# A two-layer decoder trunk: score products of two heads in the two row halves of TensorE, and SwiGLU products grouped by width

## The chip, the cores and the metric

The program runs on one core of one Trainium2 chip. The metric is the device time of one execution in microseconds (us); less is better. Every time below is taken from the runs or from the hardware profile of the kernel before the change.

## What is computed

Two consecutive decoder layers over 256 positions and a model width of 1024. Layer 0 mixes block-sparse and dilated attention, layer 1 uses a three-branch attention (compressed, selected blocks, sliding window); after each attention come a SwiGLU block and a gated per-layer embedding. The part that the change touches:

```python
def _swiglu(x, wg, wu, wd):
    return (jax.nn.silu(x @ wg) * (x @ wu)) @ wd

# layer 1, 16 query heads in 4 groups, head width 64
q  = _rms(_heads(q, NSA_HEADS), qn)
ks = _rms(_heads(ks, NSA_GROUPS), kn_s)
kw = _rms(_heads(kw, NSA_GROUPS), kn_w)
s  = einsum('bghsd,bgkd->bghsk', q, k) * ATTN_SCALE + bias   # for each branch
pr = softmax(s, causal)
o  = gates[0] * o_cmp + gates[1] * o_slc + gates[2] * o_win
h  = h + o @ w_out
h  = h + _swiglu(_rms(h, norm_ffn), w_gate, w_up, w_down)
```

With 256 positions all blocks are selected, so the selected and the window branch are two causal attentions with their own keys.

## The kernel before, in words

**Precision.** Every large product is made from two halves of each operand: a number is split into `hi` (rounded to the matmul's fast 32-bit form) and `lo` (the rest), and hi·hi + hi·lo + lo·hi is summed in PSUM. Weights are loaded by SyncE in units of 512 KB into six `raw` buffers; ScalarE writes `hi`, VectorE (in layer 1 for half of some units GpSimd) writes `lo` (`emit_load`, `emit_split`, lines 98 to 130). `take` (line 189) hands a unit to the products and starts later loads and splits.

**Order of the work.** The TensorE and SyncE queues are written by hand: the program text walks through the projections in order, and after every few products `tick` (line 158) lets queued generators (`push`) place a step of side work: the norm chains, the transposes of q and k, and `attend` (line 664), which places the three parts of attention. When each may be placed is set by a model clock and by the table `KN` of delays. The queues of VectorE, ScalarE and GpSimd are ordered by the framework's scheduler. Each queue runs in order, so a step of side work that isn't ready holds everything behind it.

**Layer 1 attention.** `q_split` and `k_split` (lines 864 to 886) normalise 8 heads at a time: `norm_twice` writes every head twice side by side, `split_t` transposes 128 columns of this at a time (128x128 transposes into the tile `qps`), so that both partition halves hold the same head, and writes q as hi over lo on the 128 partitions (`QS`) and two forms of k (`KK`). `attn1` (line 999) then has three parts. `A(i)` makes all scores of one head: two products with 256 columns (queries 0 to 127) and two with 512 (queries 128 to 255), each over all 128 rows of the array; VectorE adds the bias and takes the maximum (`neg_scores`, line 474), ScalarE takes the exponential, VectorE and GpSimd scale. `B(i)` transposes the probabilities of one head (six 128x128 transposes, tile `t`), ScalarE or VectorE copies them out of PSUM. `C(k)` makes the outputs of a pair of heads (tile `o`, 20 recorded products). `cmp_scores(b)` (line 965, tile `cs`) makes the compressed-branch scores of 8 heads. Heads 0 to 7 go first, then heads 8 to 15, whose attention waits until output pair 3 is out. The filler between these steps is the rest of the input projection (`ic`, products of 512, 304 or 256 columns), the embedding projection (`pa`) and the output projection (`oc`, 192 products of 256 columns in layer 1, of which 48 wait for the last output pair).

**SwiGLU.** `mm_units_t` and `block_step` (lines 234 to 255): for a block of 128 output features the hi weights meet hi and lo of the input side by side (one product of 512 columns) and then the lo weights meet hi (256 columns), into the same PSUM bank. The two alternate. `ga` is the gate, `ua` the up, `da` the down projection; there are 1024 such pairs in the two layers. Layer 0's scores (`attn0`, tile `s`) already use 64-row products in the two row halves, in plain 32-bit, each recorded as two passes.

Of the kernel before, what the change touches and what calls it, by code (L numbers as in the profile page):

```python
# [35 lines left out]
KN = {'stF': 7.12, 'stP': 6.0, 'st0': 1.48, 'st1': 11.0, 'sq': 3, 'LSb': 2, 'warm': 4, 'spF': 6.77, 'spP': 5.23, 'burst': 6, 'prep0': 2.6, 'prep1': 2.0, 'qk': 11.39, 'qk2': 12.0, 'qk3': 9.53, 'qk4': 13.44, 'ev': 0.63, 'gap0': 1.54, 'gap1': 2.4, 'LB0': 7.35, 'LB1': 7.66, 'LC': 2.13, 'hT': 5.0, 'cmp': 12.0, 'ev1': 1.5, 'c0': 4.0, 'c00': 0.5, 'c1': 4.5, 'c2': 9.0, 'ns': 'PPVV', 'lop': 2, 'ptd': 1, 'pb': 1}  # L36
# [3 lines left out]
def trunk(ctx: ExitStack, tc: tile.TileContext, a, out):  # L40
# [20 lines left out]
    def big(i, dt):  # L61
        return fix.tile([128, (16, 16, 12)[i] * S], dt, tag=f"big{i}", name=f"big{i}")
# [26 lines left out]
    def plan(name, w, k0, nk, c0, N):  # L89

        pieces = [(c0, N)] if isinstance(c0, int) else c0
        rows = w[k0 * 128:(k0 + nk) * 128].rearrange("(k p) n -> p k n", p=128)
        units.append((name, [(rows[:, :, c:c + n], n) for c, n in pieces], nk, sum(n for _, n in pieces)))
# [4 lines left out]
    def emit_load():  # L98
        i = ws["ld"]
        if i >= len(units):  # L100
            return
        _, aps, nk, N = units[i]
        r = wp.tile([128, 1024], F32, tag="raw", name="raw", bufs=NRAW)
        raws[i] = r
        c = 0
        for ap, n in aps:
            nc.sync.dma_start(out=r[:, :nk * N].rearrange("p (k n) -> p k n", k=nk)[:, :, c:c + n], in_=ap)
            c += n
        ws["ld"] += 1
# [124 lines left out]
    def block_step(ks, k, b, blk, x, kx, start, stop):  # L234
# [3 lines left out]
        if c is None:  # L238
            mm(t[:, 0:2 * S], hi, both.rearrange("p e s -> p (e s)"), start, False)
            mm(t[:, S:2 * S], lo, both[:, 0, :], False, stop)  # L240
        else:
            o = t[:, c:c + S]
            mm(o, hi, both[:, 0, :], start and c == 0, False)
            mm(o, hi, both[:, 1, :], False, False)
# [74 lines left out]
    plan_out(a["w_out_nsa"][0])  # L319
# [38 lines left out]
    def load_tb(tb, i):  # L358
        nc.sync.dma_start(out=tb[:, 4 * i:4 * i + 4], in_=a["tb"][:, 4 * i:4 * i + 4])
# [186 lines left out]
    def ffn(l, slot):  # L546
        nslot = 1 - slot
        hh = [big(i, F32R).rearrange("p (f e s) -> p f e s", e=2, s=S) for i in range(3)]

        def hh_pair(f, e):  # L550

            return hh[f // 8][:, f % 8:f % 8 + 2, e, :]

        def hh_both(f):
            return hh[f // 8][:, f % 8]
# [108 lines left out]
    def attend(n, A, B, C, gap, lb, p0, ready=(), pb=3, ptb=4, per_pt=1, per_a=1):  # L664

        tA, tB, k = [], [], 0
        while 2 * k < n:
# [18 lines left out]
    big0, big1, big2 = (big(i, F32) for i in range(3))  # L686
    qT = big0[:, 0:2048].rearrange("p (a s) -> p a s", s=S)
    kT = big0[:, 2048:4096].rearrange("p (a s) -> p a s", s=S)
    TB = big1.rearrange("p (h j) -> p h j", h=16)
# [21 lines left out]
    def attn0(h0):  # L711
# [4 lines left out]
        def A(k):  # L716
# [10 lines left out]
            for e, x0, x1, n in parts:  # L727
                neg_scores(p[:, e, x0:x1], s[e][:, x0:x1], TB[:, 2 * pr + e, 256 - (x1 - x0):256], nm[:, n:n + 1])
# [46 lines left out]
    def dil_bias(i):  # L775
        load_tb(TB, i)
        for k in range(4 * i, 4 * i + 4, 2):
            nc.gpsimd.tensor_tensor(TB[:, k:k + 2, :], TB[:, k:k + 2, :], lc[:, None, :].to_broadcast([128, 2, 256]), op=OP.add)
# [4 lines left out]
    load_tb(TB, 0)  # L783
    load_tb(TB, 1)
# [17 lines left out]
    QS = big(0, F32R).rearrange("p (h s) -> p h s", s=S)  # L802
    KK = big(1, F32R).rearrange("p (e g b s) -> p e g b s", e=2, g=4, b=2)
# [9 lines left out]
    KCT = fix.tile([128, 4, 2, 16], F32R, name="kct")  # L813
    TB = []

    def load_tb1():

        t = wk.tile([128, 2, 256], F32, tag="tb", name="tb", bufs=4)
        nc.sync.dma_start(out=t, in_=a["tb"][:, 2 * len(TB):2 * len(TB) + 2])
# [18 lines left out]
    def norm_twice(accs, mul):  # L838
# [3 lines left out]
        for b in range(2):  # L842
            for t in range(2):
                q = wk_tile("qn")
                src = accs[t][:, b * 256:b * 256 + 256].rearrange("p (h d) -> p h d", d=64)
                nc.vector.tensor_tensor(q.rearrange("p (h e d) -> p h e d", e=2, d=64),
                                        src[:, :, None, :].to_broadcast([128, 4, 2, 64]),
                                        comb[:, t, 4 * b:4 * b + 4, None, None].to_broadcast([128, 4, 2, 64]), op=OP.mult)
                res.append(q)
        return res  # L850

    def split_t(qn, h, gcol, hi, lo_at, lo):

        p = st_tile("qps")
        for e in range(2):
            for t in range(2):
                tr(p[:, e * 256 + t * 128:e * 256 + (t + 1) * 128],
                   qn[2 * (h // 4) + t][:, (h % 4 + e) * 128:(h % 4 + e) * 128 + 128])
# [3 lines left out]
        nc.vector.scalar_tensor_tensor(lo, pv[lo_at:], g[lo_at:], hi[lo_at:].bitcast(F32), op0=OP.mult, op1=OP.subtract)  # L862

    def k_split(accs):

        kn = norm_twice(accs, 1.0)

        def gen():
            for h in range(0, 8, 2):
                br, g = h // 4, h % 4  # L870
                split_t(kn, h, 5 + br, KK[:, 0, g:g + 2, br, :], 0, KK[:, 1, g:g + 2, br, :])
                yield KN["ev"] if g else 0.0
# [3 lines left out]
    def q_split(accs, h0):  # L876

        qn = norm_twice(accs, 64.0)

        def gen():  # L880
            for h in range(0, 8, 2):
# [6 lines left out]
    def compress(idr):  # L888
# [71 lines left out]
        pv = bass.AP(tensor=p.tensor, offset=p.offset, ap=[p.ap[0], [15, 4], [1, 16]])  # L960
        nc.scalar.activation(KCT[:, :, 0, :], pv, AF.Identity, scale=g)
        nc.vector.scalar_tensor_tensor(KCT[:, :, 1, :], pv, g, KCT[:, :, 0, :].bitcast(F32), op0=OP.mult, op1=OP.subtract)
        ev["kc"] = clk[0] + 0.8

    def cmp_scores(b):
        if b == 0:
            nc.gpsimd.memset(PC, 0.0)
        p = st_tile("cs")
        pv = p.rearrange("p (t h e c) -> p t h e c", t=2, h=8, e=2)
        for i in range(8):  # L970
            hd = 8 * b + i
            for t in range(2):
                mm(pv[:, t, i], QS[:, hd, t * 128:(t + 1) * 128], KCT[:, hd // 4], start=True, stop=True)
# [4 lines left out]
        nc.vector.tensor_tensor(sc, pv[:, :, :, 0, 0:15], tcv[:, :, 8 * b:8 * b + 8, :], op=OP.add)  # L978
        nc.vector.tensor_tensor(sc, pv[:, :, :, 1, 0:15], sc, op=OP.add)
# [19 lines left out]
    def attn1(h0):  # L999
# [3 lines left out]
        def A(i):  # L1003
            hd = h0 + i
            g = hd // 4
            s0, s1 = st_tile("s0"), st_tile("s1")
            for e in range(2):
                mm(s0[:, 0:256], QS[:, hd, 0:128], KK[:, e, g, :, 0:128], start=e == 0, stop=e == 1)
            for e in range(2):
                mm(s1, QS[:, hd, 128:256], KK[:, e, g], start=e == 0, stop=e == 1)  # L1010
            p = wk.tile([128, 768], F32, tag="p", name="p1", bufs=3)
            nm, l, r = small("nm", (128, 4)), small("l", (128, 4)), small("rl", (128, 4))
            for n, (x0, x1) in enumerate(cuts):
                src = s0[:, x0:x1] if n < 2 else s1[:, x0 - 256:x1 - 256]
                neg_scores(p[:, x0:x1], src, TB[hd // 2][:, hd % 2, 256 - (x1 - x0):256], nm[:, n:n + 1])
            if hd % 2 and len(TB) < 8:
                load_tb1()
            for n, (x0, x1) in enumerate(cuts):
                nc.scalar.activation(p[:, x0:x1], p[:, x0:x1], AF.Exp, bias=nm[:, n:n + 1], scale=-1.0,  # L1019
                                     accum_out=l[:, n:n + 1])  # L1020
            nc.vector.reciprocal(r, l)
            nc.vector.tensor_tensor(r.rearrange("p (t b) -> p t b", t=2), r.rearrange("p (t b) -> p t b", t=2), G[:, :, hd, 1:3], op=OP.mult)
            for n, (x0, x1) in enumerate(cuts):
                if KN["ns"][n] == "A":
                    nc.scalar.activation(p[:, x0:x1], p[:, x0:x1], AF.Copy, scale=r[:, n:n + 1])
                    continue
                e = nc.gpsimd if KN["ns"][n] == "P" else nc.vector
                e.tensor_scalar(p[:, x0:x1], p[:, x0:x1], r[:, n:n + 1], None, op0=OP.mult)
            stt["p", i] = p
# [14 lines left out]
        def C(k):  # L1044
            pts = [stt.pop(("pt", 2 * k + e)) for e in range(2)]
            o = ps.tile([128, 512], F32, tag="st", name="o", bufs=4)
            g = (h0 + 2 * k) // 4
            for e in range(2):
                j = (2 * k + e) % 4
# [114 lines left out]
```

## Time and profile before

| | |
|---|---|
| median of 3 runs | 712.27 us (712.05 to 712.39) |
| the profiled execution | 713.02 us, of which the span from first to last instruction is 711.2 us |
| TensorE busy in the span | 695.6 us (98%), 4386 products |
| VectorE, ScalarE, GpSimd busy | 521.9 us (73%), 413.2 us (58%), 174.2 us (24%) |
| granted TensorE clock | 1.00 (2.4 GHz) over the span |
| DMA | 121.66 MB, 171 GB/s on average |

In the profile a product is recorded with a modelled end that lies some 0.1 to 0.2 us after the next product's start; so what a product costs is read from one start to the next, and the busy share of TensorE is near 100% even where a little is lost between products. PEld is TensorE's weight load.

### The profile page before, as it was taken

The numbers are of one execution on the slowest core, as the hardware profiler recorded it, in microseconds if no ns is written. First come the engines' busy times: TensorE is split into PE (matmuls) and PEld (weight loads), VectorE is DVE, ScalarE is ACT, GpSimd is POOL, SyncE is SP. The second block draws the span as 40 slices with busy tenths as digits, with TensorE's granted clock in tenths as the row PEclk, the third lists the DMA queues.
The fourth block names the chain that finished last, engine by engine and source line by source line (L and its number), as shares of the span: only waits on it lengthen the run. The fifth ranks groups of instructions, "written<-read, shape, count | busy, mean of one in ns | idle before, by whom it ended". The sixth has DMA issues, their size and how long they took to land.

```text
span 711.2 us, 11962 instructions
## 1 busy us (share of the span) xinstructions
PE 695.6 (98%) x4386; PEld 600.9 (84%) x4386; DVE 521.9 (73%) x979; ACT 413.2 (58%) x766; POOL 174.2 (24%) x287
## 2 busy tenths in 40 slices
PE   8999999999999999999999999999999999999996
PEld 6887789888888888889878878877988888888896
DVE  5769674888877764667877897786697878847475
ACT  7547785656565653554654787686465655545342
POOL 1254200342132310001172535341232321300010
PEclk9999999999999999999999999999999999999999
DMA  8956433456647555547763245313557555655611
GB/s 304 323 181 222 163 117 114 147 172 193 202 154 217 179 197 192 192 149 229 220 214 109 97 141 180 126 31 90 156 171 230 178 183 179 206 181 176 207 60 59
DMA packets 68779, 121.66 MB, mean 171 GB/s; under 512 B 5360, under 2 KB 15472, under 8 KB 68720
## 3 DMA queue, kind: packets, MB, share of 16 engines
q1 hardware_dynamic: 68720, 120.89, 52.6%
q8 instruction: 34, 0.56, 0.3%
q14 instruction: 25, 0.20, 0.1%
HBM read 119.83 MB, written 1.05 MB: 170 GB/s over the span
## 4 chain that ended last, share of the span: by engine, by line
PE 80%; DVE 8%; ACT 4%; POOL 3%; issue 3%; DMA 2%; SPq 0%; DVEq 0%; POOLq 0%; ACTq 0%
PE ua L142 18%; PE da L142 17%; PE ga L142 17%; PE oc L142 6%; PE pc L142 5%; PE ic L142 4%; DVE lo L126 3%; PE o L142 3%; PE s L142 2%; PE t L146 2%; PE pa L142 2%; PE q L142 2%; ACT p L1019 1%; ACT hi L124 1%; PE v L142 1%
## 5 line engine op out<-in xcount | busy, mean ns | idle before, releaser
L126 DVE TENSOR_TENSOR lo<-raw,hi 128x1024 fp32r<-128x1024 f32 (+2 forms) x218 | 269.9, 1249 | 111.4 <-ACT hi L124 111.2
L124 ACT ACTIVATE hi<-raw 128x1024 fp32r<-128x1024 f32 (+4 forms) x231 | 223.9, 987 | 158.4 <-PE da L142 54.2
L142 PE MATMUL ga<-x,hi 128*128 128x512 f32 x352 | 125.4, 399 | 1.9 <-DVE h L494 1.4
L142 PE MATMUL ua<-x,hi 128*128 128x512 f32 (+1 forms) x384 | 125.3, 379 | 0.0
L142 PE MATMUL da<-big,hi 128*128 128x512 f32 x352 | 124.5, 399 | 0.0
L142 PE MATMUL ua<-x,lo 128*128 128x256 f32 x352 | 98.9, 281 | 0.0
L142 PE MATMUL da<-big,lo 128*128 128x256 f32 x352 | 98.9, 281 | 0.0
L142 PE MATMUL ga<-x,lo 128*128 128x256 f32 x352 | 98.9, 281 | 0.0
L142 PEld LDWEIGHTS ua<-x,hi 128*128 128x128 f32 x384 | 70.0, 188 | 15.1
L142 PEld LDWEIGHTS ga<-x,hi 128*128 128x128 f32 x352 | 66.1, 188 | 18.4 <-DVE h L494 1.8
L142 PEld LDWEIGHTS da<-big,hi 128*128 128x128 f32 x352 | 66.1, 188 | 16.6
L142 PE MATMUL ic<-hi,x 128*128 128x512 f32 (+2 forms) x256 | 78.9, 375 | 0.3 <-ACT big L1077 0.3
L142 PEld LDWEIGHTS ua<-x,lo 128*128 128x128 f32 x352 | 66.6, 189 | 0.0
L142 PEld LDWEIGHTS ga<-x,lo 128*128 128x128 f32 x352 | 66.5, 189 | 0.0
L142 PEld LDWEIGHTS da<-big,lo 128*128 128x128 f32 x352 | 66.5, 189 | 0.0
L574 POOL TENSOR_TENSOR th<-th,rfb 128x512 f32<-128x512 f32 x22 | 28.6, 1299 | 140.5 <-DVE th L573 140.5
L401 POOL TENSOR_TENSOR sum<-sum,sqj 128x512 f32<-128x512 f32 x12 | 17.2, 1436 | 176.1 <-ACT sqj L399 176.1
L142 PEld LDWEIGHTS ic<-hi,x 128*128 128x128 f32 x256 | 46.7, 188 | 9.6 <-issue 1.5
L142 PE MATMUL oc<-x,hi 128*128 128x256 f32 x256 | 48.6, 289 | 0.1
L142 PE MATMUL ic<-lo,x 128*128 128x512 f32 (+2 forms) x128 | 46.8, 366 | 0.0
L142 PE MATMUL pc<-x,hi 128*128 128x256 f32 x256 | 46.6, 284 | 0.0
L142 PEld LDWEIGHTS oc<-x,hi 128*128 128x128 f32 x256 | 39.8, 191 | 2.1 <-issue 1.5
(191 smaller groups left out, 1142.9 us busy)
## 6 DMA issues: line engine op xcount, KB each, us to landing
raw<-in_w_ffn_gate_dram SPq DMA_DIRECT2D x44, 512.0 KB, 3.6
raw<-in_w_ffn_up_dram SPq DMA_DIRECT2D x44, 512.0 KB, 4.2
raw<-in_w_ffn_down_dram SPq DMA_DIRECT2D x44, 512.0 KB, 3.3
raw<-in_w_in_ab_dram SPq DMA_DIRECT2D x23, 512.0 KB, 6.4
raw<-in_w_ple_gate_dram SPq DMA_DIRECT2D x16, 512.0 KB, 3.3
raw<-in_w_in_nsa_dram SPq DMA_DIRECT2D x12, 512.0 KB, 5.1
raw<-in_w_out_ab_dram SPq DMA_DIRECT2D x8, 512.0 KB, 3.3
raw<-in_w_in_nsa_dram SPq DMA_DIRECT2D x16, 256.0 KB, 4.2
```

What stands on the lines that cost most here:

```text
L124: nc.scalar.activation(hi[:, x:x + m], r[:, x:x + m], AF.Copy)
L126: e.tensor_tensor(lo[:, x:x + m], r[:, x:x + m], hi[:, x:x + m].bitcast(F32), op=OP.subtract)
L142: nc.tensor.matmul(o, l, r, start=start, stop=stop)
L146: nc.tensor.transpose(o, i, ident if idn is None else idn)
L401: e.tensor_tensor(st["sum"], st["sum"], j, op=OP.add)
L574: nc.gpsimd.tensor_tensor(v2(th), v2(th), r2(), op=OP.mult)
L1019: nc.scalar.activation(p[:, x0:x1], p[:, x0:x1], AF.Exp, bias=nm[:, n:n + 1], scale=-1.0, accum_out=l[:, n:n + 1])
```

## The change

Layer 1 attention: q is written with head j in partitions 0 to 63 and head j+4 in partitions 64 to 127 (`pairs_norm`, `split_t`), hi and lo apart, k likewise with two groups. `A` is called once per half of the queries for a pair of heads: three products for each head (hi·hi, lo·hi, hi·lo), each over 64 rows, the two heads in turn; 256 columns in the first step of a pair, 512 in the second. `attend` places these steps; two more probability tiles lie in a fourth large buffer, and two delays (`ev1`, `ev2`) are set anew. The output weights are loaded in the order of the pairs, in two loads of 64 partitions. `cmp_scores` follows the new layout. SwiGLU: in a run of products (eight pairs of a unit, or four pairs of a block at the end of an accumulation) all 512-column products come first, then all 256-column ones.

```diff
-'ev1': 1.5,
+'ev1': 1.0, 'ev2': 1.8,
...
+    def plan_pairs(name, w, m, c0, N):
+        aps = []
+        for e in range(2):
+            r = (m // 4 * 8 + 4 * e + m % 4) * 64
+            aps.append((w[r:r + 128, c0:c0 + N].rearrange("(k p) n -> p k n", p=64), slice(64 * e, 64 * e + 64), slice(0, N)))
+        units.append((name, aps, 2, N))
...
     def mm_units_t(name, n, blks, x, kx, first, last):
         ks, N = take(name, n)
         nb, nk = N // 128, len(ks)
         order = [(k, b) for b in range(nb) for k in range(nk)] if last else [(k, b) for k in range(nk) for b in range(nb)]
-        for i, (k, b) in enumerate(order):
-            block_step(ks, k, b, blks[b], x, kx, first and k == 0, last and k == nk - 1 and blks[b][1] != 0)
-            if i % 4 == 3:
-                tick()
+        run = nk if last else len(order)
+        n = 0
+        for i in range(0, len(order), run):
+            for part in ("hi", "lo") if any(blks[b][1] is None for _, b in order[i:i + run]) else (None,):
+                for k, b in order[i:i + run]:
+                    p = part if blks[b][1] is None else None
+                    if p or part != "hi":
+                        block_step(ks, k, b, blks[b], x, kx, first and k == 0,
+                                   last and k == nk - 1 and blks[b][1] != 0, p)
+                        n += 1
+                        if n % 4 == 0:
+                            tick()
...
-            elif len(tA) < n and len(tA) - len(tB) <= (pb - 1) * per_a and (not tA or now >= tA[-1] + gap * per_a):
-                A(len(tA) // per_a)
-                tA += [clk[0] + 0.5 * KN["gap0"] * i for i in range(per_a)]
+            elif len(tA) < n and (steps % 2 or len(tA) - len(tB) <= (pb - 1) * per_a) and now >= tS:
+                A(steps)
+                steps += 1
+                tS = clk[0] + gap
+                if per_s == 1 or steps % 2 == 0:
+                    tS = clk[0] + gap * per_a / per_s
+                    tA += [clk[0] + 0.5 * KN["gap0"] * i for i in range(per_a)]
...
-            for h in range(0, 8, 2):
-                dst = QS[:, h0 + h:h0 + h + 2, :]
-                split_t(qn, h, 4, dst, 64, dst[64:])
-                yield KN["ev"] if h % 4 else 0.0
+            for i in range(0, 4, 2):
+                m = h0 // 2 + i
+                split_t(qn, i, 4, QP[:, 0, m:m + 2, :], QP[:, 1, m:m + 2, :])
+                yield KN["ev"] if i else 0.0
...
         def A(i):
-            hd = h0 + i
-            g = hd // 4
-            s0, s1 = st_tile("s0"), st_tile("s1")
-            for e in range(2):
-                mm(s0[:, 0:256], QS[:, hd, 0:128], KK[:, e, g, :, 0:128], start=e == 0, stop=e == 1)
-            for e in range(2):
-                mm(s1, QS[:, hd, 128:256], KK[:, e, g], start=e == 0, stop=e == 1)
+            m, t, b = h0 // 2 + i // 2, i % 2, h0 // 8
+            hds = (h0 + i // 2, h0 + i // 2 + 4)
+            n = 128 * (t + 1)
+            s = [st_tile("s") for _ in range(2)]
+            for x, (ql, kl) in enumerate(((0, 0), (1, 0), (0, 1))):
+                for e in range(2):
+                    o = slice(64 * e, 64 * e + 64)
+                    mm(s[e][:, 0:2 * n], QP[o, ql, m, t * 128:(t + 1) * 128], KP[o, kl, b, :, 0:n], start=x == 0, stop=x == 2)
...
-    push(seq(after([], [q0] + ks), attend(8, *attn1(0), KN["gap1"], KN["LB1"], 0, ready=("cmp0", "vw"))))
+    push(seq(after([], [q0] + ks), wait(KN['ev2']), attend(8, *attn1(0), KN["gap1"], KN["LB1"], 0, ready=("cmp0", "vw"), pb=2, per_a=2, per_s=2)))
...
-    push(seq(after(["o3"], [q1]), attend(8, *attn1(8), KN["gap1"], KN["LB1"], 4, ready=("cmp1",))))
+    push(seq(after(["o3"], [q1]), wait(KN["ev2"]), attend(8, *attn1(8), KN["gap1"], KN["LB1"], 4, ready=("cmp1",), pb=2, per_a=2, per_s=2)))
```

How the queues move. First TensorE's queue where layer 1's SwiGLU begins (`ga<-x,hi` is the 512-column product, `ga<-x,lo` the 256-column one); before:

```order
L142 MATMUL ga<-x_5513,hi 128x512
L142 MATMUL ga<-x_5513,lo 128x256
L142 MATMUL ga<-x_5513,hi 128x512
L142 MATMUL ga<-x_5513,lo 128x256
L142 MATMUL ga<-x_5513,hi 128x512
```

and now:

```order
L153 MATMUL ga<-x_5503,hi 128x512 x8
L153 MATMUL ga<-x_5503,lo 128x256 x8
L153 MATMUL ga<-x_5503,hi 128x512 x8
L153 MATMUL ga<-x_5503,lo 128x256 x8
```

A width now stays for eight products (four at the end of an accumulation) instead of one.

Second, TensorE's queue where the attention of heads 8 to 15 begins (`o` the last output pair of the first eight heads, `oc` the output projection, `s` the scores, `cs` and `pcp` the compressed branch); before:

```order
L142 MATMUL o<-pt_4918,big_3619 64x128
L142 MATMUL oc_4872<-x_4219,hi 128x256 x2
L142 MATMUL oc_4872<-x_4219,lo 128x256
L142 MATMUL oc_4872<-x_4219,hi 128x256 x2
L142 MATMUL oc_4872<-x_4219,lo 128x256
L142 MATMUL oc_4873<-x_4219,hi 128x256 x2
L142 MATMUL oc_4873<-x_4219,lo 128x256
L142 MATMUL oc_4873<-x_4219,hi 128x256 x2
L142 MATMUL oc_4873<-x_4219,lo 128x256
L142 MATMUL s_4988<-big_3618,big_3617 128x256 x2
L142 MATMUL s_4989<-big_3618,big_3617 128x512 x2
L142 MATMUL cs<-kct,big_3617 128x32 x16
```

and now, the end of the 36 `oc` products that stand between that output pair and the first score step, and what follows:

```order
L153 MATMUL oc_4787<-x_4201,lo 128x256
L153 MATMUL s<-big_3620,big_3619 128x256 x6
L157 MATMUL pcp<-ident,big_3622 128x128 x4
L153 MATMUL oc_4786<-x_4201,hi 128x256 x2
L153 MATMUL oc_4786<-x_4201,lo 128x256
L153 MATMUL oc_4786<-x_4201,hi 128x256 x2
L153 MATMUL oc_4786<-x_4201,lo 128x256
L153 MATMUL oc_4787<-x_4201,hi 128x256 x2
L153 MATMUL oc_4787<-x_4201,lo 128x256
L153 MATMUL oc_4787<-x_4201,hi 128x256 x2
L153 MATMUL oc_4787<-x_4201,lo 128x256
L153 MATMUL s<-big_3620,big_3619 128x512 x6
```

Before the first score step of heads 8 to 15 stood 48 of the 192 `oc` products of the layer, now 84; and the 16 `cs` products now stand ahead of it, behind it before. Behind these rows come two more score steps without anything between them, then twelve transposes.

## Rows read from the trace of the kernel before

**Rows 1.** The page: busy us of each engine (share of the span) xinstructions.
```profile
PE 695.6 (98%) x4386; PEld 600.9 (84%) x4386; DVE 521.9 (73%) x979; ACT 413.2 (58%) x766; POOL 174.2 (24%) x287
```

**Rows 2.** Windows of layer 1's attention: us, then busy of PE, PEld, DVE, ACT, POOL.
```profile
399.29:449.51 50.22, 49.67 (x363) 41.89 (x363) 41.72 (x141) 38.13 (x110) 20.38 (x34) 1.00 0.40 137
...
449.51:473.04 23.53, 21.84 (x168) 17.51 (x167) 20.24 (x98) 19.01 (x69) 10.42 (x14) 1.00 0.22 68
```

**Rows 3.** Timeline of PE in the down projection: start, length, instruction; nine pairs.
```profile
299.61 0.40 PE L142 MATMUL da<-big,hi 128*128 128x512 f32 x1
...
302.44 0.40 PE L142 MATMUL da<-big,hi 128*128 128x512 f32 x1
```

**Rows 4.** Timeline of PE, input projection: a run of 54 products; then four after a break.
```profile
31.16 0.39 PE L142 MATMUL ic<-hi,x 128*128 128x512 f32 x1
...
43.18 0.39 PE L142 MATMUL ic<-hi,x 128*128 128x512 f32 x1
...
65.25 0.39 PE L142 MATMUL ic<-lo,x 128*128 128x512 f32 x1
...
66.64 0.39 PE L142 MATMUL ic<-lo,x 128*128 128x512 f32 x1
```

**Rows 5.** Timeline of PE, embedding gate: a run of 256-column products, 45 between two rows.
```profile
325.07 0.28 PE L142 MATMUL pc<-x,lo 128*128 128x256 f32 x1
...
330.47 0.28 PE L142 MATMUL pc<-x,lo 128*128 128x256 f32 x1
```

**Rows 6.** Timeline of PE: eight transposes of q, then a head's scores, in layer 1.
```profile
396.35 1.04 PE L146 MATMUL qps<-ident,qn 128*128 128x128 f32 x8
...
397.14 0.36 PE L142 MATMUL ic<-hi,x 128*128 128x256 f32 x1
...
400.50 0.87 PE L142 MATMUL s<-big,big 128*128 128x256 f32 x4
...
401.20 0.28 PE L142 MATMUL ic<-hi,x 128*128 128x256 f32 x1
```

**Rows 7.** Timeline, layer 0: the first two products of a score step alone.
```profile
57.53 0.38 PE L142 MATMUL s<-big 64*128 64x128 f32 x2
```

**Rows 8.** Timeline, layer 0: the whole score step between input-projection products.
```profile
57.22 0.39 PE L142 MATMUL ic<-hi,x 128*128 128x512 f32 x1
...
57.53 0.93 PE L142 MATMUL s<-big 64*128 64x128 f32 x8
...
58.39 0.50 PE L142 MATMUL ic<-hi,x 128*128 128x512 f32 x1
...
58.73 0.39 PE L142 MATMUL ic<-lo,x 128*128 128x512 f32 x1
```

**Rows 9.** Timeline of PE, heads 8 to 15: first and last scores, compressed scores, SwiGLU.
```profile
449.51 0.87 PE L142 MATMUL s<-big,big 128*128 128x256 f32 x4
...
450.22 1.85 PE L142 MATMUL cs<-kct,big 128*128 128x32 f32 x16
...
451.92 0.48 PE L142 MATMUL oc<-x,hi 128*128 128x256 f32 x2
...
473.04 1.30 PE L142 MATMUL s<-big,big 128*128 128x256 f32 x4
...
492.54 0.40 PE L142 MATMUL ga<-x,hi 128*128 128x512 f32 x1
```

**Rows 10.** Windows of the tile csw alone: VectorE's part of the compressed softmax.
```profile
449.51:473.04 23.53, 2.59 (x7) 0.40 (x1) 1.00 0.22 68
```

**Rows 11.** Timeline of PE in layer 1's attention: waits, with their releaser in brackets.
```profile
460.17 1.11 PE L142 MATMUL s<-big,big 128*128 128x256 f32 x4 [0.20 <-DVE nm L474]
...
461.46 0.99 PE L146 MATMUL t<-ident,p 128*128 128x128 f32 x6 [0.18 <-DVE nm L474]
```

**Rows 12.** Groups of VectorE for q and k, 379 to 446 us: xcount | busy us, mean ns.
```profile
L862 DVE SCALAR_TENSOR_TENSOR big<-qps,h,big 64x512 fp32r<-64x512 f32 x7 | 5.1, 757 | 0.6 <-ACT big L861 0.4
...
L846 DVE TENSOR_TENSOR qn<-ic,rs_yq 128x512 f32<-128x512 f32 x8 | 5.0, 684 | 2.2 <-POOL rs_yq L373 2.2
```

More of the change, by code (lines that the diff above doesn't have):

```diff
@@ L92, in plan @@
         rows = w[k0 * 128:(k0 + nk) * 128].rearrange("(k p) n -> p k n", p=128)
-        units.append((name, [(rows[:, :, c:c + n], n) for c, n in pieces], nk, sum(n for _, n in pieces)))
+        at = 0
+        aps = []
+        for c, n in pieces:
+            aps.append((rows[:, :, c:c + n], slice(0, 128), slice(at, at + n)))
+            at += n
+        units.append((name, aps, nk, at))
+    def plan_pairs(name, w, m, c0, N):
+        aps = []
+        for e in range(2):
+            r = (m // 4 * 8 + 4 * e + m % 4) * 64
+            aps.append((w[r:r + 128, c0:c0 + N].rearrange("(k p) n -> p k n", p=64), slice(64 * e, 64 * e + 64), slice(0, N)))
+        units.append((name, aps, 2, N))
     raws, his, los = {}, {}, {}
@@ L104, in emit_load @@
         raws[i] = r
[L105 to L108, printed above, removed]
+        for ap, ps_, cs_ in aps:
+            nc.sync.dma_start(out=r[:, :nk * N].rearrange("p (k n) -> p k n", k=nk)[ps_, :, cs_], in_=ap)
         ws["ld"] += 1
@@ L237, in block_step @@
         t, c = blk
[L238 to L244, printed above, removed]
+        o = t[:, S:2 * S] if c is None else t[:, c:c + S]
+        if part != "lo":
+            if c is None:
+                mm(t[:, 0:2 * S], hi, both.rearrange("p e s -> p (e s)"), start, False)
+            else:
+                mm(o, hi, both[:, 0, :], start and c == 0, False)
+                mm(o, hi, both[:, 1, :], False, False)
+        if part != "hi":
             mm(o, lo, both[:, 0, :], False, stop)
@@ L318, in trunk @@
         plan("pp", a["w_ple_proj"][1], 0, 2, c * 512, 512)
-    plan_out(a["w_out_nsa"][0])
+    for m in range(0, 8, 2):
+        for c in range(2):
+            plan_pairs("out", a["w_out_nsa"][0], m, c * 512, 512)
     l1_units += range(l1_0 + 8, len(units))
@@ L800, in trunk, with p_tile @@
     ple(0, 1, False)
-    QS = big(0, F32R).rearrange("p (h s) -> p h s", s=S)
-    KK = big(1, F32R).rearrange("p (e g b s) -> p e g b s", e=2, g=4, b=2)
+    QP = big(0, F32R).rearrange("p (l m s) -> p l m s", l=2, m=8)
+    KP = big(1, F32R).rearrange("p (l b r s) -> p l b r s", l=2, b=2, r=2)
+    big3 = big(3, F32)
+    pmore = [big3[:, 768 * i:768 * (i + 1)] for i in range(2)]
+    np1 = [0]
+    def p_tile():
+        i = np1[0] % 5
+        np1[0] += 1
+        return pmore[i - 3] if i > 2 else wk.tile([128, 768], F32, tag="p", name="p1", bufs=3)
     big2 = big(2, F32)
@@ L1013, in A @@
[L1013 to L1016, printed above, removed]
+            m, t, b = h0 // 2 + i // 2, i % 2, h0 // 8
[3 more added lines that the diff above has]
+            for x, (ql, kl) in enumerate(((0, 0), (1, 0), (0, 1))):
+                for e in range(2):
+                    o = slice(64 * e, 64 * e + 64)
+                    mm(s[e][:, 0:2 * n], QP[o, ql, m, t * 128:(t + 1) * 128], KP[o, kl, b, :, 0:n], start=x == 0, stop=x == 2)
@@ new lines, in A @@
+            if t == 0:
+                for e in range(2):
+                    stt["p", i + e] = p_tile()
+            p = [stt["p", i - t + e] for e in range(2)]
+            nm, l, r = small("nm", (128, 4)), small("l", (128, 4)), small("rl", (128, 4))
+            parts = [(p[e][:, 256 * t + n * br:256 * t + n * (br + 1)], s[e][:, n * br:n * (br + 1)], TB[m][:, e, 256 - n:256], 2 * e + br)
+                     for e in range(2) for br in range(2)]
+            for x, src, tb, c in parts:
+                neg_scores(x, src, tb, nm[:, c:c + 1])
```

136 lines of the change are left out of this document (72 added, 64 removed).

## The prediction

> **What bounds the kernel now.** I read the page first: TensorE is busy for 695.6 of 711.2 us, the next engine, VectorE, for 521.9 [rows 1]. So two things alone can move the time: what TensorE has to do, read from one start to the next in its timeline, and the few places in which it waits. The waits are in layer 1's attention, so I read that in windows: while heads 0 to 7 are at work (399.29 to 449.51 us) VectorE is busy for 41.72 of 50.22 us; from the first to the last scores of heads 8 to 15 it is busy for 20.24 of 23.53, 86%, and TensorE's rows there wait for VectorE's maximum `nm` [rows 2, 11]. That last stretch is as long as VectorE makes it; in the rest of the program TensorE sets the pace.
>
> The profiled execution took 713.02 us, 1.8 more than its span, and lies 0.75 above the median of 712.27; I make the sum as a difference and put it on the median. A measurement of this kernel tells apart about 0.2%, 1.4 us: "no change" is 710.85 to 713.69.
>
> **SwiGLU, 1024 pairs.** Now eight pairs take 302.44 - 299.61 = 2.83 us, 0.354 a pair [rows 3]. What a product costs when its width does not change is seen elsewhere: 512 columns take (43.18 - 31.16) / 53 = 0.227 us in a long run, and (66.64 - 65.25) / 6 = 0.232 in the first six after a break [rows 4]; 256 columns take 5.40 / 45 = 0.120 [rows 5]. The bounds of the gain: with the steady pace from the first product on, a pair costs 0.347, and 1024 x 0.0068 = 7.0 us are saved; if each 512-column product keeps what it costs beside a 256-column one (0.354 - 0.120 = 0.234), nothing is. The new runs are eight long for 608 pairs and four long for 416. A run of eight starts after a change of width, so I take four products at 0.232 and four at 0.227, and 0.119 for the 256 columns, between 0.120 and the 0.118 that the pair leaves: 2.79 against 2.83, 0.04 saved; a run of four, all of it at 0.232, saves some 0.01. 76 x 0.04 + 104 x 0.01 = 4.1; as runs of eight in VectorE's busy stretches will hold less well, **-3.5 us**. Rows 4 have the weights as the moving operand, here it is the input; rows 5, with the input moving, show the same 13 ns over the bare columns, so I carry the pace over.
>
> TensorE's weight loads bear on this. In rows 4 a product of 512 columns starts 14 ns after the bare 0.213 us, so the load of the next weights lies under it, over the full array. The Trainium skill ("TensorE: Matmul & The Clock Gate", section "The mechanism") says that a weight load overlaps running products only where the row group differs; by it the load is paid in any order and this term is 0, an estimate of 715.9 where the sum below has 712.4 without it. The trace speaks against it.
>
> **Transposes, 24 fewer of 128x128 for q and k.** Eight take 397.14 - 396.35 = 0.79 us [rows 6]: **-2.4 us**, all on TensorE before heads 8 to 15. VectorE loses six operations of 0.68 and six of 0.76 there [rows 12].
>
> **Scores.** A head now takes 401.20 - 400.50 = 0.70 us [rows 6]. No row shows the new form, 64-row products in the fast 32-bit form. The nearest is layer 0's step: its first two products, one for each row half, are over within 0.38 us of the same start [rows 7], so the halves run side by side. But the step is dear to enter and to leave: its predecessor starts at 57.22 and the step at 57.53, 0.08 more than the 0.227 of a 512-column product; its first pair of products waits for its own weights, about 0.11; the drain behind it costs about 0.09; and the first product behind takes 58.73 - 58.39 = 0.34, 0.11 over 0.227 [rows 8, 4]. Some 0.4 us for each visit, none of which the full-array step pays. Streams side by side take 3 x 0.120 = 0.36 and 3 x 0.23 = 0.69. For heads 0 to 7: 4 x 0.36 + 4 x 0.69 + 8 x 0.4 = 7.4 against 8 x 0.70 = 5.6; one step stands right behind an output pair, which pays the entry anyway: **+1.6 us**. If the halves ran one after another it would be 4.2 more; without the cost of a visit, 1.4 less than now. Heads 8 to 15 have the same excess, and it lies under VectorE there: nothing.
>
> The Trainium skill ("TensorEngine Tiling (Array Packing)", section "Theoretical Speedup") gives up to 2x where 64 rows suffice. An estimate by it: half of 5.6 us, -2.8 where I have +1.6, and 710.0 in all. Layer 0's rows do not bear it out: the visit costs as much as it saves.
>
> **Filler moved ahead.** Before the first scores of heads 8 to 15 there were 48 `oc` products, now 84: 36 x 0.120 = **+4.3 us** [rows 5]. The 16 `cs` products, 451.92 - 450.22 = 1.70 us [rows 9], now stand ahead as well: **+1.7**. They are the same work; moving it matters, since what follows cannot shrink by it. The stretch from first to last scores took 473.04 - 449.51 = 23.53 us with VectorE at 86% [rows 9, 2]; it loses of VectorE's work only the compressed softmax, 2.59 us on `csw` and some 0.7 on its small tiles: **-3.3** [rows 10]. Three score steps now stand together there with no filler. From the last scores to SwiGLU is 492.54 - 473.04 = 19.5 us, and one more head's six transposes stands in it: **+0.7**.
>
> **New waits with heads 0 to 7.** Score steps now come in pairs and transposes by twelve, with fewer products between; each step still takes two of four PSUM tiles, which VectorE has to read first. What is queued behind a step that waits is everything: `ic`, `pa`, `oc`. The rows of the later stretch, where this is already so, show 0.2 us at a time, more with what the modelled ends hide [rows 11]. I count six places at half a microsecond: **+3.0**; bounds -1.1 (the 0.55 us idle in this window and as much just before it go away) and +5.
>
> The two loads for each unit of output weights, the more frequent placing of side work in SwiGLU and the new tiles I count at nothing: weights are loaded five units ahead, no side work stands in the middle of SwiGLU, and the tiles replace others. Without that cover a late unit would show as a wait of `oc` for `hi`.
>
> Sum: -3.5 - 2.4 + 1.6 + 4.3 + 1.7 - 3.3 + 0.7 + 3.0 = +2.1; 713.02 + 2.1 = 715.1 for the profiled execution, **714.4 us** on the median.
>
> **Rivals.**
> - *VectorE's relief shows* (faster). Its 12 operations fewer, some 8.6 us of 41.72 [rows 12, 2], end the waits with heads 0 to 7 instead of adding any: -1.1 in place of +3.0, 710.3 us. For it: those waits name VectorE. Against: the order is written ahead, and steps in pairs ask for more at once. It decides if TensorE idles under 1.5 us in that window. With the steady pace in SwiGLU as well, 706.8. Chance 0.22.
> - *Waits stay as they are*, +1 in place of +3: 712.4, no change. 0.16.
> - *Grouping gives nothing*, each product of 512 keeping 0.234: 717.9. The skill's rule on loads would come to the same. 0.14.
> - *Row halves in turn*, not side by side, in the fast form: 4.2 more with heads 0 to 7, 718.6. For it: layer 0 shows only the plain form. 0.08.
> - *Halving without a price for the visit*, 710.0, as the tiling page has it: 0.04.
> - The forecast: 0.36, of which a quarter falls below 713.69.
>
> **How the numbers follow.** Slower: 0.27 + 0.14 + 0.08, and 0.02 of the rest: 0.51. Same: 0.16 + 0.09 = 0.25. Faster: 0.22 + 0.04, less the 0.02: 0.24. The range takes in the halves in turn at the top and, below, the relief together with two thirds of the steady pace: 708 to 719 us. Since cases of both signs hold much, the likeliest one's own range is 713 to 716.5.
>
> **What would show it.** Right: 512-column products of SwiGLU near 0.23 us and pairs near 0.35; score steps beginning 7 ns apart in the halves, with some 0.1 us lost on each side; the first scores of heads 8 to 15 some 8 us later against the start of the layer, SwiGLU some 5 to 6. Wrong: SwiGLU shorter by over 6 us, the stretch of heads 8 to 15 below 19 us, or TensorE without waits with heads 0 to 7.

## The result, and the profile after

| | before | after |
|---|---|---|
| median | 712.33 us (712.05 to 712.44, 4 runs) | 720.89 us (719.14 to 722.53, 4 runs) |
| profiled execution, span | 713.02, 711.2 us | 721.34, 719.6 us |
| granted TensorE clock, mean | 1.00 | 0.990 |

The change makes the kernel slower: the ratio is 1.0123, with a 95% interval of 1.011 to 1.0136. That is 8.6 us where 2.1 were forecast, and 1.9 us above the top of the range. The four runs after differ by 3.4 us, those before by 0.4; their mean clocks are 0.990, 0.988, 0.992 and 0.992, for 721.34, 722.53, 720.44 and 719.14 us.

Of the page, the engines' busy time (against [rows 1]), and the granted clock in 40 slices, of which one has fallen:

```profile
PE 697.9 (97%) x4394; PEld 601.4 (84%) x4394; DVE 510.3 (71%) x973; ACT 411.9 (57%) x761; POOL 179.2 (25%) x287
...
PEclk9999999999999999999999999979999999999999
```

Windows of layer 1's attention (us, busy time of PE, PEld, DVE, ACT, POOL, then granted clock, DMA share, GB/s): from the first scores of heads 0 to 7 to the first of heads 8 to 15, from there to the last score step, and on to SwiGLU.

```profile
397.58:459.06 61.48, 56.12 (x401) 44.65 (x400) 42.60 (x152) 38.46 (x109) 21.86 (x33) 0.97 0.45 121
459.06:482.20 23.14, 19.23 (x125) 12.85 (x124) 15.73 (x85) 16.47 (x64) 9.00 (x13) 0.78 0.16 47
482.20:502.52 20.32, 20.16 (x168) 17.21 (x167) 11.22 (x29) 11.66 (x30) 2.34 (x4) 1.00 0.18 52
```

Against [rows 2, 9] the first stretch has grown from 49.01 us (400.50 to 449.51) to 61.48, the second has barely shrunk, from 23.53 to 23.14, and the third went from 19.50 to 20.32. TensorE's idle time in the first two is 5.36 and 3.91 us, 0.55 and 1.69 before; VectorE's share in the second is 68%, where it was 86%. So VectorE fills less of the second stretch than before, though most of TensorE's waits there still name it (1.94, 0.74, 0.22 and two of 0.2 us). What is new is in the clock's column: 0.97 and 0.78.

TensorE's timeline shows the three places. First, the transposes of head 1 and the score step behind them (the idle time and its releaser in brackets):

```profile
416.48 0.52 PE L157 MATMUL t<-ident,p 128*128 128x128 f32 x3 [0.60 <-DVE nm L498]
417.55 0.52 PE L157 MATMUL t<-ident,p 128*128 128x128 f32 x3 [0.54 <-DVE rl L1081]
419.07 1.10 PE L153 MATMUL s<-big,big 64*128 64x256 f32 x6 [1.01 <-ACT pt L1097]
```

The maximum `nm`, on which the first of these waits is put, stands in VectorE's queue behind a low half, and that low half waits for a load. ScalarE's and VectorE's rows in front of it:

```profile
413.33 1.06 ACT L135 ACTIVATE hi<-raw 128x1024 fp32r<-128x1024 f32 x1 [2.81 <-DMA raw<-in_w_out_nsa_dram]
...
414.43 1.23 DVE L137 TENSOR_TENSOR lo<-raw,hi 128x1024 fp32r<-128x1024 f32 x1 [1.18 <-ACT hi L135]
```

ScalarE stands still for 2.81 us until the first unit of output weights has landed, and VectorE for 1.18 us behind it. In the kernel before no wait of ScalarE is put to these weights.

Second, the output projection, which needs the output pair's result `x` from VectorE:

```profile
435.13 0.28 PE L153 MATMUL oc<-x,hi 128*128 128x256 f32 x1
437.48 0.39 PE L153 MATMUL oc<-x,hi 128*128 128x256 f32 x1 [2.08 <-DVE x L495]
...
438.89 1.45 PE L157 MATMUL t<-ident,big 128*128 128x128 f32 x6
440.14 1.49 PE L157 MATMUL t<-ident,p 128*128 128x128 f32 x6
441.56 1.31 PE L153 MATMUL s<-big,big 64*128 64x512 f32 x6
...
443.21 0.48 PE L153 MATMUL oc<-x,hi 128*128 128x256 f32 x2
```

Third, the score steps that stand together at the start of heads 8 to 15:

```profile
463.68 0.47 PE L153 MATMUL s<-big,big 64*128 64x512 f32 x1 [0.74 <-DVE nm L498]
464.37 0.92 PE L153 MATMUL s<-big,big 64*128 64x512 f32 x5 [0.22 <-DVE nm L498]
...
467.63 2.61 PE L157 MATMUL t<-ident,big 128*128 128x128 f32 x11 [1.94 <-DVE big L1085]
470.16 1.01 PE L153 MATMUL s<-big,big 64*128 64x256 f32 x6
...
472.15 2.83 PE L153 MATMUL o<-pt,big 128*64 128x256 f32 x16
474.90 1.65 PE L153 MATMUL s<-big,big 64*128 64x512 f32 x6
476.48 0.87 PE L157 MATMUL t<-ident,p 128*128 128x128 f32 x6
```

Behind the second and the third wait TensorE runs slowly without waiting for anything. Behind the second this begins 1.4 us after the wait's end, with six transposes that take 440.14 - 438.89 = 1.25 us, where eight took 0.79 in [rows 6]; from 467.63 to 476.48 everything is slow, the 16 products of an output pair among it (2.75 us to the next start). The granted clock is 0.50, which is 1.2 GHz of 2.4, from 438.95 to 442.30 and from 467.63 to 476.45. Behind the first place, waits of 0.60, 0.54 and 1.01 us, the clock stayed up.

SwiGLU's pace in runs of eight is as forecast. Timeline of the down projection, eight pairs:

```profile
296.40 2.00 PE L153 MATMUL da<-big,hi 128*128 128x512 f32 x8
298.24 1.11 PE L153 MATMUL da<-big,lo 128*128 128x256 f32 x8
299.19 2.00 PE L153 MATMUL da<-big,hi 128*128 128x512 f32 x8
```

Eight pairs take 2.79 us, 2.83 in [rows 3], the 512-column products 1.84 / 8 = 0.230 each.

### The profile page after: what moved, and what is told of

Read it like the earlier page. It is cut to its first block, busy times and chain, and to the rows that moved or that the text cites. A ratio compares the mean times of both kernels' runs of the same rounds, so it can differ in the third digit from the quotient of the medians.

```text
span 719.6 us, 12008 instructions
## 1 busy us (share of the span) xinstructions
PE 697.9 (97%) x4394; PEld 601.4 (84%) x4394; DVE 510.3 (71%) x973; ACT 411.9 (57%) x761; POOL 179.2 (25%) x287
## 4 chain that ended last, share of the span: by engine, by line
PE 80%; DVE 7%; ACT 4%; POOL 3%; DMA 3%; issue 2%; SPq 1%; DVEq 0%; ACTq 0%; POOLq 0%
PE ua L153 17%; PE ga L153 17%; PE da L153 17%; PE oc L153 5%; PE ic L153 5%; PE pc L153 4%; PE o L153 3%; DVE lo L137 2%; PE t L157 2%; PE s L153 2%; PE pa L153 2%; ACT hi L135 2%; PE q L153 2%; PE v L153 1%; DMA raw<-in_w_in_ab_dram 1%
## 5 line engine op out<-in xcount | busy, mean ns | idle before, releaser
L153 PE MATMUL ua<-x,hi 128*128 128x512 f32 (+1 forms) x384 | 96.1, 375 | 0.0
L153 PE MATMUL ga<-x,hi 128*128 128x512 f32 x352 | 92.9, 395 | 2.3 <-DVE h L518 1.8
L153 PE MATMUL da<-big,hi 128*128 128x512 f32 x352 | 89.6, 393 | 0.0
L153 PE MATMUL ua<-x,lo 128*128 128x256 f32 x352 | 57.1, 282 | 0.0
L153 PEld LDWEIGHTS ua<-x,lo 128*128 128x128 f32 x352 | 52.7, 189 | 5.1
L153 PEld LDWEIGHTS ga<-x,lo 128*128 128x128 f32 x352 | 51.0, 190 | 5.5
L153 PEld LDWEIGHTS da<-big,lo 128*128 128x128 f32 x352 | 49.1, 190 | 4.2
L153 PE MATMUL ga<-x,lo 128*128 128x256 f32 x352 | 52.5, 281 | 0.0
L153 PE MATMUL da<-big,lo 128*128 128x256 f32 x352 | 50.3, 282 | 0.0
L610 POOL TENSOR_TENSOR th<-us,th 128x512 f32<-128x512 f32 x20 | 36.3, 1816 | 37.8 <-DVE us L568 37.8
```

The lines of the kernel that those rows point to most:

```text
L153: nc.tensor.matmul(o, l, r, start=start, stop=stop)
L610: nc.gpsimd.tensor_tensor(y, x, y, op=OP.mult)
```

## The experiments

Two theories stood against each other at first. One: the order of the change makes TensorE stand still, the clock falls to its lower level behind such a wait, and the fall costs as much as the waits. The other: the clock falls because of the 64-row products themselves, whatever the waits.

**The grouping alone**, in the kernel before: `block_step` and `mm_units_t` taken from the change, nothing else.

> The kernel before with the grouped SwiGLU alone. Theory (the grouping is worth what the two traces show in the SwiGLU stages, 1.39 us in layer 0 and 1.38 us less its start in layer 1, and all of the loss lies in layer 1's attention): 709.5 us, between 708.5 and 710.5, granted clock 1.00, 512-column products pitched near 0.230 us. Rival (SwiGLU is shorter after the change only because its inputs are ready earlier, or because VectorE has less to do): no change, 712.3 us.

Measured: 709.65 us (708.41 to 710.18), ratio 0.9961, interval 0.9949 to 0.9974; clock 1.00. Layer 1's attention is what it was, by the windows of its first and second stretch:

```profile
397.54:446.57 49.03, 48.47 (x354) 40.68 (x353) 40.52 (x140) 37.23 (x108) 19.66 (x32) 1.00 0.43 140
446.57:470.10 23.53, 21.84 (x168) 17.51 (x167) 20.26 (x98) 19.02 (x69) 10.36 (x14) 1.00 0.23 68
```

49.03 and 23.53 us against 49.01 and 23.53. So the grouping is worth 2.6 us in the kernel before, and this half of the change by itself is faster than either kernel. It is the fastest version of this study.

**The waits filled.** Products with zero weights are put into a sum that is open anyway, behind the twelfth product of the output projection and ahead of the first transposes of heads 8 to 15.

```diff
+FILL = (16, 16)
...
+        for _ in range(n if pad else 0):
+            nc.tensor.matmul(pad["t"][:, 0:256], pad["z"], pad["x"], start=False, stop=False)
...
+                            if first and n == 4 and not pad.get("done"):
+                                pad["done"] = 1
+                                fill(FILL[0])
...
         def B(i):
+            if h0 == 8 and i == 0:
+                fill(FILL[1])
```

> The changed kernel with 32 products of 256 columns added, zero weights into an open sum: 16 behind the twelfth product of the output projection, where TensorE waited 2.08 us, and 16 ahead of the first transposes of heads 8 to 15, where it waited 0.74, 0.22 and 1.94 us. They take some 3.8 us in all and need nothing that is late. Theory (TensorE stands still there, the granted clock falls to its lower level behind each wait, and that costs 5.8 us): the clock stays at 1.00, and the time falls by some 5 us, to 715 or 716 us, though there are more products. Rival one (the clock falls because of the 64-row products, which are all still there): the clock falls as before, 721 us. Rival two (TensorE is not really standing still in those waits): 3.8 us longer, 725 us.

Measured: 718.87 us (718.77 to 719.09), ratio 1.0095, interval 1.0081 to 1.0109; mean clock 0.995. At the third place, the timeline:

```profile
466.62 2.19 PE L266 MATMUL oc<-big,zero 128*128 128x256 f32 x16
468.64 1.80 PE L158 MATMUL t<-ident,big 128*128 128x128 f32 x12
470.38 1.02 PE L154 MATMUL s<-big,big 64*128 64x256 f32 x6
...
471.91 1.52 PE L154 MATMUL o<-pt,big 128*64 128x256 f32 x16
```

Twelve transposes now take 1.74 us, where eleven took 2.53, and the 16 products 1.45 instead of 2.75: full speed, with every 64-row product still there. That tells against the second theory. But the time fell by 2 us only, since the first place, which was not filled, now has a fall behind it:

```profile
417.26 0.52 PE L158 MATMUL t<-ident,p 128*128 128x128 f32 x3 [1.11 <-DVE nm L511]
418.33 0.52 PE L158 MATMUL t<-ident,p 128*128 128x128 f32 x3 [0.54 <-DVE rl L1097]
419.85 1.49 PE L154 MATMUL s<-big,big 64*128 64x256 f32 x6 [1.00 <-ACT pt L1115]
421.27 0.79 PE L154 MATMUL pa<-px,hi 128*128 128x256 f32 x2
```

Its first wait grew from 0.60 to 1.11 us, by as much as ScalarE's wait for the output weights, 3.32 us here and 2.81 in the change; VectorE's queue has the same order in both. The next products are slow: a pair of `pa` products takes 421.86 - 421.27 = 0.59 us, 0.34 in the change.

**All three filled**: twenty more zero products ahead of the transposes of head 1.

> The kernel of the second run with twenty more zero products (12 and 8, into a sum that the embedding projection then starts anew) ahead of the transposes of head 1, where TensorE waited 1.11 and 0.54 us and the clock fell behind. Theory (every fall of the clock stands behind waits): clock 1.00 throughout, and 2.5 to 3.2 us less than the second run's 718.9, so 715.5 to 716.5 us. Rival (the falls move on to another place when one is filled, as that of the first run of heads 0 to 7 seemed to do): clock below 1.00 and 718 us or more.

Measured: 716.62 us (716.16 to 717.82), ratio 1.0068, interval 1.0056 to 1.0081; clock 1.00 throughout. By windows of the first two stretches:

```profile
398.05:458.63 60.58, 58.48 (x438) 47.72 (x437) 41.91 (x152) 38.09 (x109) 20.52 (x33) 1.00 0.46 122
458.63:477.90 19.27, 17.38 (x139) 12.31 (x138) 15.26 (x85) 16.10 (x65) 9.03 (x13) 1.00 0.19 56
```

With 52 more products (some 52 x 0.12 = 6.2 us of work, in place of 0.60, 0.54, 2.08 and 1.94 us of waiting) the kernel is 4.3 us faster than the change as it stands; set each against the kernel before measured beside it (711.90 and 712.33), and it is 3.8. In the two profiles layer 1's attention takes 162.24 us with the falls and 157.47 without them: the falls cost 4.8 us. From the rows themselves: 438.89 to 443.21 took 4.32 us and takes 2.92 in this run, 1.4 less; 467.63 to 476.48 took 8.85, and the same products 5.49 here, 3.4 less (one transpose of 0.11 us, which stands there in addition, is taken off). The sum is the same 4.8.

**A wait made in the kernel before**, which has none of the change's products.

```diff
             p = stt.pop(("p", i))
+            if h0 == 8 and i == 0:
+                for _ in range(6):
+                    nc.vector.tensor_scalar(p, p, 1.0, None, op0=OP.mult)
```

> The kernel before, with nothing of the change, and six multiplications by 1.0 of the probabilities of head 8 on VectorE (128x768 each, in place) ahead of that head's transposes, so that TensorE must wait there some 3.5 us longer. Theory (a wait of this size brings the clock to its lower level, whatever products stand around it): granted clock below 1.00 with the low stretch behind the wait, and 3 to 4 us on top of the wait: 718.5 to 720 us. Rival (the clock falls with the 64-row score products): clock 1.00, the wait alone, 715 to 716 us.

Measured: 718.17 us (717.79 to 718.59) against 711.90 for the kernel before beside it, ratio 1.0088, interval 1.0072 to 1.0103; mean clock 0.994. The timeline around the wait:

```profile
463.94 1.51 PE L146 MATMUL t<-ident,p 128*128 128x128 f32 x6 [5.45 <-DVE p L1035]
465.11 1.63 PE L142 MATMUL s<-big,big 128*128 128x256 f32 x4
466.53 1.48 PE L146 MATMUL t<-ident,p 128*128 128x128 f32 x6
467.81 0.90 PE L146 MATMUL pcp<-ident,big 128*128 128x128 f32 x4
```

The full-array scores behind it take 466.53 - 465.11 = 1.42 us, 0.70 in [rows 6], and six transposes 1.28, where eight took 0.79. So a fall needs no 64-row product. Its price is smaller than expected: the six transposes, the scores and the six transposes up to 467.81 take 3.87 us, about 2.0 at full clock, so some 1.9 of the 6.3 us are the clock's and most of the rest is the wait.

**Real work instead of zeros.** Two delays of the order are changed.

```diff
-'LB1': 7.66, ... 'ev2': 1.8,
+'LB1': 9.5, ... 'ev2': 3.5,
```

> The changed kernel with two of its delays altered, and nothing else: the attention's start behind its last condition from 1.8 to 3.5 us, and the time from a pair's scores to its transposes from 7.66 to 9.5 us, so that more of the real products stand between a pair's scores and its transposes. Theory (the loss is waits and what the clock does behind them, both a matter of the order; the 64-row products by themselves cost nothing that counts): waits shorter by 2 to 3 us, one fall of the clock fewer or none, 714 to 717 us. Rival (VectorE's work for two heads at once is the bound, whatever the order): the waits only move, within 1.5 us of 721.

Measured: 718.10 us (717.11 to 719.59), ratio 1.0088, interval 1.0074 to 1.0102; mean clock 0.988. That is 2.8 us better than the change (2.4 with each against the kernel before beside it), and neither expectation came out. Windows of the two places where the clock is down:

```profile
420.00:430.00 10.00, 8.97 (x51) 6.09 (x50) 5.33 (x17) 6.44 (x19) 4.47 (x11) 0.69 0.35 79
...
465.00:470.00 5.00, 3.59 (x16) 2.97 (x18) 4.84 (x23) 4.76 (x19) 3.83 (x7) 0.50 0.11 39
```

The largest waits are shorter (1.6, 0.8, 0.7 and 0.7 us), but there are more of them close together, and the clock falls twice all the same, the first time behind 0.29, 0.71 and 0.32 us. So the order moves the time; this order does not avoid the falls, and one that does was not found.

**SwiGLU alternating again**, with the rest of the change.

> The changed kernel with SwiGLU's products alternating as in the kernel before. Theory (the grouping gives 2.8 us, and layer 1's attention does not depend on it): 723.7 us, 723 to 724.5. Rival (the grouping's larger steps hurt somewhere else, so that the sum of the two changes is not the sum of their parts): within 1 us of 721, or below it.

Measured: 725.14 us (724.09 to 726.43), ratio 1.0179, interval 1.0163 to 1.0195; mean clock 0.984. That is 4.2 us more than the change, outside both expectations. In the profiled executions it is 4.7: 2.9 because the SwiGLU stages are back at their lengths, and 1.8 in layer 1's attention, 164.02 us, where the waits of head 1 have become 1.42, 0.55 and 0.89 us and the clock falls among them too. The wait of the output projection is down to 0.80 us, and no fall follows it.

There is also a fall that no long wait explains:

```profile
401.49 1.93 PE L153 MATMUL cs<-kct,big 128*128 128x64 f32 x16 [0.42 <-DVE kct L1000]
...
405.16 1.65 PE L153 MATMUL s<-big,big 64*128 64x512 f32 x6
```

The score step is recorded with 1.65 us, 0.97 in the change, and the granted clock from 404.40 to 407.70 is 0.50. What stands ahead of it is one wait of 0.42 us, the 16 products `cs` of 64 columns, and a microsecond of 512-column products at clock 1.00. In the change the same `cs` products stand behind the same wait of 0.42 us and the clock stays up. So falls come where TensorE has waited, but the length of a wait does not settle whether one comes. The two halves of the change don't simply add up: the clock falls nowhere with the grouping alone, twice in the change and three times here.

**The row halves one head after the other**, within a score step.

```diff
-            for x, (ql, kl) in enumerate(((0, 0), (1, 0), (0, 1))):
-                for e in range(2):
+            for e in range(2):
+                for x, (ql, kl) in enumerate(((0, 0), (1, 0), (0, 1))):
```

> The changed kernel with the six products of a score step in another order: the three of one head (partitions 0 to 63), then the three of the other, instead of the two in turn. Theory (the two row halves work side by side, but only products that follow one another closely do): a step of 256 columns grows from 0.55 us to some 0.75, one of 512 from 0.89 to some 1.35, and the kernel by 3 to 6 us with the waits, 724 to 727 us. Rival (the order within a step makes no difference, since the halves take their products from separate queues, or since they do not overlap in the first place): steps of 0.55 and 0.89 us and 721 us.

Measured: 722.06 us (720.47 to 723.39), ratio 1.0142, interval 1.0124 to 1.016, not to be told from the change's. The theory fell here: the steps did not grow. One of its score steps, in the timeline:

```profile
403.57 0.97 PE L153 MATMUL s<-big,big 64*128 64x512 f32 x6
404.48 0.50 PE L153 MATMUL ic<-hi,x 128*128 128x512 f32 x1
```

0.91 us against 0.89 (and 0.56 against 0.55 with 256 columns). One after another, three products of 512 columns and then three more would take 6 x 0.227 = 1.36. So products of the two row halves run side by side although three of the one half stand ahead of the first of the other.

**No low halves on GpSimd** (`'lop': 0`), after two odd rows in VectorE's queue. VectorE's and GpSimd's timeline of the change ahead of the second wait (`x<-o,x` is what the output projection waits for):

```profile
434.01 1.64 DVE L1085 TENSOR_SCALAR p<-p,rl 128x256 f32<-128x256 f32 x2
...
437.01 0.41 DVE L495 TENSOR_TENSOR x<-o,x 128x256 fp32r<-128x256 f32 x1
```

```profile
434.15 1.35 POOL L137 TENSOR_TENSOR lo<-raw,hi 128x512 fp32r<-128x512 f32 x1 [5.43 <-ACT hi L135]
```

> The changed kernel with VectorE making the low halves of all units, none on GpSimd. In the changed kernel two of VectorE's 64 scalings of the probabilities took 1.37 and 1.38 us instead of 0.28 to 0.47, both while GpSimd's subtraction for a low half ran, and both ahead of a wait of TensorE (1.01 us of the scores of head 2, 2.08 us of the output projection). Theory (that subtraction holds VectorE off): no scaling longer than 0.47 us, those two waits shorter by up to 1 us each, against some 0.7 us more on VectorE for each low half that it takes over: 719 to 722 us. Rival (the two long scalings have another cause): they stay, and VectorE's added work makes 722 us or more.

Measured: 723.54 us (720.75 to 727.06), ratio 1.0176, interval 1.0134 to 1.0218. VectorE's scalings of `p` in the change and in this run (minimum, median and longest in ns):

```profile
L1085 DVE TENSOR_SCALAR p<-p,rl x20: 337/349/1381, 411.1 to 487.3; 128x256 f32<-128x256 f32 x20
```

```profile
L1085 DVE TENSOR_SCALAR p<-p,rl x20: 344/348/495, 411.5 to 487.3; 128x256 f32<-128x256 f32 x20
```

The longest falls from 1381 to 495 ns (the trace has 32 such scalings on VectorE, not 64): GpSimd's subtraction held VectorE's scaling for about 1 us. What that cost is not shown. The output projection no longer waits here, but with the halves one after the other it does not wait either, and there a scaling did take 1372 ns; and the scores of head 2 still wait 0.91 us, 1.01 in the change. The time did not fall: VectorE has the subtractions to do itself, TensorE waits in other places (1.15 us ahead of `cs`, 1.25 ahead of head 1's transposes), and two falls of the clock remain.

## Why the prediction was wrong

The direction was right, the size was not: 2.1 us forecast, 8.3 between the profiled executions. By its steps:

- **What bounds the kernel**: right that SwiGLU and layer 1's attention are where the time moves. Wrong in what a wait costs: every duration was taken at the full clock, since the profile before shows 1.00 everywhere.
- **SwiGLU, -3.5**: -2.6 by its own run. Runs of eight gave the 0.04 us that were worked out; 76 of them make 3.0, so the runs of four gave nothing or a little less. The rival that grouping gives nothing is out. (The estimate beside this term, 715.9 against 712.4 without it, does not follow from the prediction's own sum: without the term 714.4 becomes 717.9, as its list of rivals has it.)
- **Transposes, -2.4**: from the layer's start to its first scores 59.00 us became 57.30, -1.7, where 16 of the 24 stand (-1.6). That the two agree is in part luck: 12 more products of `ic` stand there (1.1 us of busy time), and TensorE idles 1.1 us less (2.04 to 0.91).
- **Scores, +1.6**: right in the two steps read, part by part. By the timeline of the change,

```profile
403.23 0.39 PE L153 MATMUL ic<-hi,x 128*128 128x512 f32 x1
403.55 0.97 PE L153 MATMUL s<-big,big 64*128 64x512 f32 x6
404.44 0.50 PE L153 MATMUL ic<-hi,x 128*128 128x512 f32 x1
404.78 0.40 PE L153 MATMUL ic<-lo,x 128*128 128x512 f32 x1
...
407.39 0.62 PE L153 MATMUL s<-big,big 64*128 64x256 f32 x6
407.94 0.50 PE L153 MATMUL ic<-hi,x 128*128 128x512 f32 x1
```

  a step of 512 columns costs 0.32 - 0.23 ahead of it, 0.89 - 0.69 within it, and 0.34 - 0.23 behind it, 0.40 in all for the visit; one of 256 gives 0.39 likewise. The forecast had 0.4. The halves run side by side in the fast form, so that rival is out, and a visit does have its price.
- **Filler moved ahead, +6.0, and the second stretch, -3.3**: without the fall of the clock the second stretch takes 19.27 us, even with zero products in its waits, where the forecast gives 23.53 - 3.3 = 20.2. With the fall it takes 23.14. So without the fall it shrank by somewhat more than forecast, and the fall took nearly all of that back. Heads 8 to 15 begin 10.8 us later against the start of the layer, where 8 were forecast, and SwiGLU 11.2, where 5 to 6 were.
- **New waits, +3.0, six places of half a microsecond**: this is the step that failed, twice. TensorE's idle time with heads 0 to 7 grew by 5.36 - 0.55 = 4.8 us, near the upper bound of 5, and most of it lies in two places of about 2 us each instead of six small ones. [rows 11], 0.2 us each, were a poor measure: they come from single heads, and the same stretch of the kernel before has a wait of 1.11 us that the prediction passed over:

```profile
464.78 0.65 PE L142 MATMUL o<-big 15*64 15x256 f32 x4 [1.11 <-ACT big L996]
```

  And behind the second and the third of the large waits the clock falls to half, which costs 4.8 us more. No term and no rival had that.
- **Output weights in two loads, put at nothing**: this cover failed too. The first unit came late, and not as a wait of `oc` for `hi`: ScalarE waited 2.81 us for it, with VectorE's maxima and TensorE's transposes of head 1 queued behind. That chain is read from the trace, and borne out by the run with two waits filled, where ScalarE waited 0.51 us longer and the transposes did too. No run loads these weights earlier or in one piece, so the price of it is open.

The terms with what was measured in their place: 2.1 + 0.9 (SwiGLU) + 4.8 (clock) leaves 0.5 of the 8.3 for the waits and all the rest. That it is so little is partly luck: TensorE's idle time grew by 4.8 us with heads 0 to 7 and by 2.2 behind them, and shrank by 1.1 ahead of them. With the clock held at 1.00 by the zero products the change comes out at 716.6 us, inside the range. The rival of VectorE's relief is out: VectorE has 11.6 us less to do, and TensorE waits for it more; by the trace, because its work for two heads arrives at once and stands in a queue ahead of what TensorE needs next, and because that queue itself stands behind a late load.

The Trainium skill ("TensorE: Matmul & The Clock Gate", section "HAM oscillation — how this bites in real kernels") tells of a kernel in which TensorE waits for a DMA, is throttled, and starts its next batch slowly, so that the waits and the slow starts are both paid. The runs here agree in that: 4.8 us behind waits of 2.08 and 0.74 + 0.22 + 1.94 us, and none once these are filled. The waits of the kernel in the Trainium skill are some 3 to 5 us long; here shorter ones did it.

Open is what decides whether a wait brings the clock down, and what else than the order could avoid the waits. That VectorE's queue (16 maxima of four steps ahead of the scaling on which the first transposes wait) is the cause of the third is read from the trace, not tried.

## What to carry to other kernels

Price a new wait of TensorE at its own length and at what the products behind it lose if the clock falls; the profile before, at 1.00 all through, gave no warning of one. Filling a wait with products that need nothing is a quick test of that: here two runs told the clock's 4.8 us from the rest. Follow a wait back through every queue, too: the first of these ended at a load that ScalarE waited for. And measure the separable halves of a change apart: one of these two was worth keeping alone.

## What the hardware showed unexpectedly

- Waits of 0.60, 0.54 and 1.01 us in a row left the clock up; with waits of 1.11, 0.54 and 1.00 at the same place it fell, and the scores and `pa` products there took 2.5 us more (6.43 against 3.89). But it also fell behind 0.29, 0.71 and 0.32 us, and behind 0.42 alone where the same 0.42 had left it up. So a shift of half a microsecond went with a loss of some 3 us, and no run here gives a rule for it. That this is why the change's runs differ by 3.4 us is likely, but only one of them was profiled.
- Products of the two row halves overlap whichever way they are interleaved: 0.89 us in turn, 0.91 one head after the other.
- A scaling on VectorE that starts while GpSimd subtracts two tensors of 128x512 ends 0.15 us behind it: 1.37 and 1.38 us instead of 0.35. One that had begun before the subtraction took its 0.35. GpSimd's own scalings beside it do no such thing: in the kernel before none of VectorE's 32 scalings of `p` took over 0.47 us.
